# adaLN row products in four column groups of TensorE, and the S5 projection from the first stage on

## Chip, cores, metric

One core of a Trainium2 chip runs the whole layer as one program. The metric is the device time of one execution in microseconds (us), lower is better. The engines are named as in the profile: PE (TensorE), DVE (VectorE), ACT (ScalarE), POOL (GpSimd), and SP, which issues most DMAs. PEld is PE's loading of stationary operands.

## The reference, cut to what matters

The layer takes 512 latent tokens and 256 context tokens of width 2048, all float32. `mod = silu(c) @ ada_w + ada_b` gives six vectors of 2048 for the latent stream: shift and scale of the first norm, gate `g1`, shift and scale of the second norm, gate `g2`. `mod_c`, from `c_ctx`, gives the first two for the context. `ada_w` is 2048 x 12288, so each vector is a row product: one row (or two) against a 2048 x 2048 matrix.

```
h  = modulate(rmsnorm(x), sh1, sc1)                  # 512 x 2048
p  = h @ w_in                                        # S5 takes columns 0:1024, Hyena 1024:4096
ugc = modulate(rmsnorm(ctx), csh1, csc1) @ w_in[:, :1024]
mix = [rmsnorm(S5(p, ugc)), rmsnorm(Hyena(p))]
x  = x + g1 * (mix @ w_out)
h2 = modulate(rmsnorm(x), sh2, sc2)
x  = x + g2 * (silu(h2 @ wg) * (h2 @ wu)) @ wd       # inner width 5632
out = rmsnorm(x)
```

S5 is a diagonal complex scan over the tokens in both directions, Hyena two gated long convolutions by FFT, here by matrix products.

## The kernel before, in words

Activations lie feature-major: a tile is 128 features x 512 tokens. Large products are made in three float32r passes (`mm3`, lines 136-139): weights and activations are split into a high and a low part (`wsplit`, lines 122-134: ACT copies, DVE subtracts), and high-high, high-low and low-high are added in PSUM. Weights come through one `Stream` (lines 141-175): chunks of 512 KB in a fixed order, four raw buffers, loaded by SP three to four chunks ahead, split one ahead.

PE's order is that of the program. Side work is written as generators that yield a cost; `pump(gen, budget)` (lines 188-195) adds the budget to a credit and steps the generator until the credit is used up. The constants `PUMP_...` set how much side work follows each chunk.

The stages in order:

1. **ada** (lines 797-811). For j in 0..3 and kind in 0..1, `ada_block` (760-788) takes 8 chunks of `ada_w`, 2 row tiles (k) of 512 columns each, and makes one matmul for each k (line 766): stationary `sil[:, k, :]` (128 x 2, the silu of c and c_ctx), moving the weights (128 x 512 float32), out 2 x 512. The result is copied by ACT (773) and turned to columns by four small matmuls (778). After each j, `modulate` (790-793) makes the high and low parts of four feature tiles of latent (`hhi`, `hlo`) and context (`chi`, `clo`). Pumped beside: `x_side` (loads and transposes x and ctx, squares, stores `xd`) and `s5_mats`, whose loop b (432-443) makes the S5 input matrices: DVE products, PE transposes into an `ax` PSUM tile, ACT copies into `bm` (one buffer), store to `bmd` by SP.
2. **S5 projection** (868-886): four groups of 256 columns of `w_in`; for each k and 128 columns an "item" of six matmuls, three on 512 latent tokens and three on 256 context tokens, 128 items in all. Pumped beside: the second half of `s5_mats` (448-500), the filter features (503-545), and `late`.
3. **Hyena projection** (1098-1118): 6 groups x 8 chunks x 24 matmuls. Beside it `gen`: the S5 chain (scan on DVE), then `filters`; and `late`.
4. **GLU** (1302-1327): 4 groups x 4 chunks x 24 matmuls, with the rest of `gen`, then `hyena_all`, and `late`.
5. **w_out**, two halves (1336-1391), with `hyena_all` and `late` in the first.
6. **FFN** (1428-1457): gate and up products, then down products, in chunks of eight 128-wide slices; `late` for `g2` in the first chunk.

`late` is `ada_late` (826-862): the other four vectors for the latent stream only (g1, sh2, sc2 by line 865, g2 by line 1409). It has 256 tiles of 128 x 512 of `ada_w`, loaded by SP into three buffers (`araw`, line 835). DVE multiplies each by the scalar `sil[:, k, 0]` and adds it to `acc` (844, 846); after 16 tiles PE sums over the partitions with `ones` (854).

PSUM has eight banks: the pool `mm` has five, `ax` three.

Of the kernel before, what the change touches and what calls it, by code (L numbers as in the profile page):

```python
# [20 lines left out]
L = 512  # L21
# [22 lines left out]
PUMP_BL = 1.8  # L44
PUMP_B = 5.986
PUMP_C = 4.2
PUMP_CL = 1.102
# [4 lines left out]
PUMP_DL = 0.875  # L52
PUMP_EL = 0.619
PUMP_SL = 0.648
PUMP_SC = 0.018
PUMP_FL = 1.826
NRAW = 3
LAG = 0.47
# [14 lines left out]
def kernel(  # L73
# [26 lines left out]
    kp.tile([128, 56], F32, name="padl")  # L100
# [163 lines left out]
    sil = kp.tile([128, KT, 2], F32, name="sil")  # L264
# [48 lines left out]
    def s5_mats():  # L313
# [118 lines left out]
        for b in range(16):  # L432
# [9 lines left out]
            SY.dma_start(bmd[b], bm)  # L442
            yield 3.1
# [22 lines left out]
        for b in range(16):  # L466
# [17 lines left out]
            for gh in range(2):  # L484
# [9 lines left out]
                V.tensor_tensor(out=zg[:, :, 7 * C:8 * C], in0=pz[:C, :, :C], in1=zg[:, :, 7 * C:8 * C], op=ALU.add)  # L494
            zs = Z[:, :, 7 * C:8 * C]
            V.tensor_tensor(out=zs, in0=zs, in1=di, op=ALU.add)
            SY.dma_start(zd[:, gs, :], Z)
            yield 4.4
# [50 lines left out]
    def filters():  # L549
# [112 lines left out]
        for n in range(8):  # L662
# [7 lines left out]
            pump_late(PUMP_SL)  # L670
# [4 lines left out]
            pump_late(PUMP_SL)  # L675
# [21 lines left out]
    rsx = hp.tile([128, L], F32, tag="acc", name="rsx", bufs=1)  # L697
    rsc = hcp.tile([128, CL], F32, tag="rsc", name="rsc", bufs=1)

    def x_side():  # L700
# [12 lines left out]
        for qd in range(4):  # L713
# [5 lines left out]
            for kk in range(4):  # L719
# [6 lines left out]
                SY.dma_start(xd[k], t)  # L726
# [33 lines left out]
    def ada_block(kind, j):  # L760
        ps = mmt(f"ada{kind}_{j}")
        for kc in range(8):
            rw = ws.next()
            for i in range(2):
                k = kc * 2 + i
                T.matmul(ps[:2, :], lhsT=sil[:, k, :], rhs=rw[:, i, :], start=(k == 0), stop=(k == KT - 1))  # L766
            if kc == 2:
                while todo:
                    todo.pop(0)()
            pump(xs, PUMP_X)  # L770
            pump(pre, PUMP_A)
        rowt = tmp(f"rowt{kind}{j}")
        S.copy(rowt[:2], ps[:2, :])

        def columns():
            pc = mmt(f"adc{kind}_{j}")
            for f in range(4):
                T.matmul(pc[:, 2 * f:2 * f + 2], lhsT=rowt[:2, f * 128:(f + 1) * 128], rhs=ident[:2, :2],
                         start=True, stop=True)
# [14 lines left out]

    xs = x_side()
    next(xs)
    for j in range(4):
        for kind in range(2):
            ada_block(kind, j)

        def mods(j=j):
            finish(xs)
            for k in range(4 * j, 4 * j + 4):
                hhi[k], hlo[k] = ht(f"hh{k}", F32R), ht(f"hl{k}", F32R)
                modulate(xT[k], mA[:, k, 0:1], mB[:, k, 0:1], rsx, hhi[k], hlo[k])
# [765 lines left out]
```

## Time and profile before

| | us |
|---|---|
| three runs | 2731.11, 2734.54, 6765.77 |
| median | 2734.54 |
| the profiled execution, device time | 2726.15 |
| its span, first to last instruction | 2724.4 |

The profiled execution is 8.4 us under the median and 5.0 under the lowest run. The page gives busy time by engine, the chain of waits that ended last, groups of instructions and DMA issues; windows give the same by stretch of time. A float32 matmul appears as two records (line 766 has 256 for 128 matmuls); a float32r matmul as one. A record's length on PE contains pipeline time: what a matmul costs in a row of them is the step from one start to the next. "Busy" of PE is therefore above the time that the matmuls need at full pace.

### The profile page before, as it was taken

Reading aid. Unit: us, or ns where it says so; the run is one execution under the profiler, and the core shown is the slowest. Engines: PE = TensorE matmul, PEld = TensorE weight load, DVE = VectorE, ACT = ScalarE, POOL = GpSimd, SP = SyncE. Lnnn points to the kernel's source line nnn. Section 1 sums busy time; section 2 is a strip of 40 time slices with the busy share of each in tenths; the row PEclk is TensorE's granted clock in tenths of the full one; section 3 lists DMA queues with packets and bytes.
Section 4 is the critical chain, followed back from the end, with each engine's and each line's share of the span. In section 5 each row is a group of like instructions: output and inputs, shape, how many; then the busy total and the mean of one; then the engine's idle time right before and its main releaser. Section 6 shows DMA issues by size and latency. Waiting matters only on the chain.

```text
span 2724.4 us, 34481 instructions
## 1 busy us (share of the span) xinstructions
PE 2631.0 (97%) x12431; PEld 2108.4 (77%) x12431; DVE 1517.3 (56%) x2666; ACT 1021.7 (38%) x1869; POOL 116.7 (4%) x143
## 2 busy tenths in 40 slices
PE   7999999999888999999999999999999999999997
PEld 2347777777677888887888888888888888888887
DVE  4779548948859999867463333332333333233338
ACT  5437554564455533233322222222222222222234
POOL 0000010011010001120000000000000000000002
PEclk9999999999999999998999999999999999999999
DMA  8987576676673477443462332333233323332324
GB/s 286 298 270 250 182 229 210 195 240 220 200 237 126 150 216 183 111 155 107 133 205 98 96 99 94 100 93 101 93 101 93 98 96 101 93 101 94 100 93 148
DMA packets 274812, 415.26 MB, mean 152 GB/s; under 512 B 27263, under 2 KB 143279, under 8 KB 274128
## 3 DMA queue, kind: packets, MB, share of 16 engines
q1 hardware_dynamic: 268400, 401.48, 45.4%
q0 software_dynamic: 5664, 10.52, 1.9%
q8 instruction: 98, 1.61, 0.2%
q10 hardware_dynamic: 576, 1.05, 0.1%
q14 instruction: 74, 0.61, 0.1%
HBM read 363.45 MB, written 49.48 MB: 152 GB/s over the span
## 4 chain that ended last, share of the span: by engine, by line
PE 79%; DVE 9%; DMA 5%; ACT 3%; issue 3%; SPq 0%; POOL 0%; DVEq 0%; ACTq 0%; POOLq 0%
PE fg L137 12%; PE fg L138 12%; PE fg L139 12%; PE fd L139 6%; PE fd L137 6%; PE fd L138 6%; PE ada L766 3%; PE wo L138 2%; PE wo L137 2%; PE wo L139 2%; DMA ar<-in_ada_w_dram 1%; PE ph L137 1%; PE ph L138 1%; PE ph L139 1%; PE hi L1219 1%
## 5 line engine op out<-in xcount | busy, mean ns | idle before, releaser
L846 DVE SCALAR_TENSOR_TENSOR acc<-ar,sil,acc 128x512 f32<-128x512 f32 x240 | 180.3, 751 | 60.3 <-DMA ar<-in_ada_w_dram 58.2
L766 PE MATMUL ada<-rad,sil 128*2 128x512 f32 x256 | 121.4, 612 | 14.1 <-DMA rad<-in_ada_w_dram 14.1
L1425 DVE SCALAR_TENSOR_TENSOR xn<-fd,modc,xn 128x512 f32<-128x512 f32 (+1 forms) x112 | 74.6, 672 | 32.3 <-PE fd L139 31.9
L766 PEld LDWEIGHTS ada<-rad,sil 128*2 128x2 f32 x256 | 18.6, 85 | 82.5 <-issue 63.8
L1132 POOL TENSOR_TENSOR sqa<-sqa,sqo 128x256 f32<-128x256 f32 x22 | 19.1, 868 | 1461.5 <-ACT sqo L1131 1460.6
L994 ACT COPY tr<-S 128x128 f32<-128x128 f32 (+1 forms) x96 | 34.0, 362 | 110.7 <-DVE S L998 109.1
L998 DVE TENSOR_REDUCE S<-tr 128x64 f32<-128x192 f32 x190 | 66.4, 350 | 10.0 <-ACT tr L994 5.1
L996 DVE TENSOR_TENSOR tr<-a,S 128x128 f32<-128x128 f32 x190 | 62.5, 329 | 7.3 <-ACT S L961 3.9
L1446 DVE TENSOR_TENSOR ft<-fs,fg 128x512 f32<-128x512 f32 x44 | 30.1, 684 | 61.1 <-PE fg L139 61.1
L1026 POOL DMA_DIRECT2D T<-zd x64 | 37.8, 615 | 532.4 <-ACT u L883 359.7
L1219 PE MATMUL hi<-kiv,cb 128*128 128x256 f32 x256 | 57.2, 380 | 0.4 <-DVE U L1191 0.4
L1219 PEld LDWEIGHTS hi<-kiv,cb 128*128 128x128 f32 x256 | 48.1, 190 | 7.4 <-issue 0.8
L1444 ACT ACTIVATE fs<-fg 128x512 f32<-128x512 f32 x44 | 26.3, 598 | 37.6 <-PE fg L139 37.6
L138 PE MATMUL hf<-zl,ffc 128*128 128x256 f32 x128 | 36.1, 284 | 1.6 <-DVE zl L184 1.6
L137 PE MATMUL hf<-zh,ffc 128*128 128x256 f32 x128 | 37.0, 291 | 0.0
L137 PE MATMUL fdf<-phf,ffc 128*128 128x256 f32 x128 | 36.3, 285 | 0.0
L138 PE MATMUL fdf<-plf,ffc 128*128 128x256 f32 x128 | 36.2, 283 | 0.0
L139 PE MATMUL fdf<-phf,ffc 128*128 128x256 f32 x128 | 36.1, 283 | 0.0
L139 PE MATMUL hf<-zh,ffc 128*128 128x256 f32 x128 | 36.0, 283 | 0.0
L954 PE MATMUL sp<-U,bml 128*128 128x96 f32 x256 | 32.8, 282 | 2.7 <-ACT U L931 2.0
L954 PEld LDWEIGHTS sp<-U,bml 128*128 128x128 f32 x256 | 31.7, 198 | 4.7 <-ACT U L931 2.5
L1449 ACT CAST gh<-ft 128x512 fp32r<-128x512 f32 x44 | 27.2, 619 | 21.6 <-DVE ft L1446 21.6
(3521 smaller groups left out, 8329.3 us busy)
## 6 DMA issues: line engine op xcount, KB each, us to landing
ar<-in_ada_w_dram SPq DMA_DIRECT2D x256, 256.0 KB, 4.0
rwd<-in_ffn_w_down_dram SPq DMA_DIRECT2D x96, 512.0 KB, 3.6
rwf<-in_ffn_w_gate_dram SPq DMA_DIRECT2D x176, 256.0 KB, 2.8
rwf<-in_ffn_w_up_dram SPq DMA_DIRECT2D x176, 256.0 KB, 3.1
rad<-in_ada_w_dram SPq DMA_DIRECT2D x64, 512.0 KB, 5.4
rwv<-in_w_in_dram SPq DMA_DIRECT2D x48, 512.0 KB, 4.9
rwo<-in_w_out_dram SPq DMA_DIRECT2D x32, 512.0 KB, 3.9
bmd<-bm SPq DMA_DIRECT2D x16, 512.0 KB, 3.2
```

The source lines that it names most:

```text
L137: T.matmul(ps, lhsT=wh, rhs=xh, start=start, stop=False)
L138: T.matmul(ps, lhsT=wh, rhs=xl, start=False, stop=False)
L139: T.matmul(ps, lhsT=wl, rhs=xh, start=False, stop=stop)
L766: T.matmul(ps[:2, :], lhsT=sil[:, k, :], rhs=rw[:, i, :], start=(k == 0), stop=(k == KT - 1))
L846: V.scalar_tensor_tensor(out=acc, in0=rw, scalar=sil[:, k, 0:1], in1=acc, op0=ALU.mult, op1=ALU.add)
L954: T.matmul(ps[:, g * NCH:(g + 1) * NCH], lhsT=bm[:, ri, g, :], rhs=U[f4][0][:, hb * 4 + g, :], start=True, stop=True)
L994: S.copy(tr[:, n0:, :, :, 2], St[:, k:k + 2 - n0])
L996: V.tensor_tensor(out=tk[:, :, :, 0:2].rearrange("p r g m -> p m r g"), in0=ac, in1=bc(St[:, k - 1], 2, 2), op=ALU.mult)
L998: V.tensor_reduce(out=St[:, k], in_=tk, op=ALU.add, axis=AX.X)
L1026: GP.dma_start(Tt[:, g, :], bass.AP(zb.tensor, zb.offset, [[C, Q], [G * 240, C], [1, 128]]))
L1219: T.matmul(ps[:, es], lhsT=cbs[s, ft][:, eo, ri, cs], rhs=kiv[:, ft, ri, es], start=(n_ == 0), stop=(n_ == 3))
L1425: V.scalar_tensor_tensor(out=xn[d_][:, cs], in0=pl[f][:, cs], scalar=modc[:, 3, d_:d_ + 1], in1=xn[d_][:, cs], op0=ALU.mult, op1=ALU.add)
```

## The change

- `row_products`: for each k, two matmuls of 256 columns take the place of one of 512. The stationary operand is `silx[:, 2k:2k+32]`, 32 columns of which the first two are wanted. The outputs of the four matmuls of a pair (k even, k odd; left and right half) go to PSUM partitions 0, 32, 64 and 96: four column groups of PE. The small column matmuls sum the two groups that belong together (`sel`).
- `late` uses the same row products: a step takes two tiles, loads two more, and yields 1.0. DVE's lines 844 and 846 and `acc` are gone. There are four `araw` buffers, and `late` starts in the Hyena projection, with one step for each chunk there, two in GLU and in the first half of w_out, one in the FFN's first chunk.
- The S5 projection is taken in two halves of 512 columns, by row tiles: `Half` holds four `mm` banks and, for the first half, two `ax` banks (for the second one `mm` and one `ax`). Two chunks of `w_in` for each of j = 1, 2, 3 come between the `ada_w` chunks; their items (four k tiles x four slices for each j, 48 of the 64 of the first half) run after the row products of `ada` steps, at most two for each step. The items of k = 12 to 15 and the second half follow as before, with `pre` pumped after every two items.
- `modulate` of a j is spread over one k for each step.
- The stores to `bmd` and `xd` are issued by ACT, not SP; `s5_mats` yields between the two halves of a b, in both its loops. `gen` gets 5.0 in place of 4.2 for each chunk of the Hyena projection.

```diff
-NRAW = 3
+NRAW = 4
-PUMP_B = 5.986
-PUMP_C = 4.2
+PUMP_B = 2.4
+PUMP_C = 5.0
...
             ws.add(f"ad{j}{kind}{kc}", (128, 2, 512), [wsrc(adw, kc * 2, 2, kind * D + j * 512, 512)], False)
-    for g in range(4):
-        for kc in range(4):
-            ws.add(f"wi{g}{kc}", (128, 4, 256), [wsrc(win, kc * 4, 4, g * 256, 256)])
+                if j and kind * 8 + kc in (5, 9):
+                    kq = (j - 1) * 4 + kind * 2
+                    ws.add(f"wi0{kq}", (128, 2, 512), [wsrc(win, kq, 2, 0, 512)])
+    for kq in (12, 14):
+        ws.add(f"wi0{kq}", (128, 2, 512), [wsrc(win, kq, 2, 0, 512)])
+    for kq in range(0, 16, 2):
+        ws.add(f"wi1{kq}", (128, 2, 512), [wsrc(win, kq, 2, 512, 512)])
...
-    sil = kp.tile([128, KT, 2], F32, name="sil")
+    silx = kp.tile([128, 64], F32, name="silx")
+    V.memset(silx, 0.0)
+    sil = silx[:, :2 * KT].rearrange("p (k v) -> p k v", v=2)
...
                 S.copy(bm[:, ri], ps.rearrange("p (g c) -> p g c", g=4))
-            SY.dma_start(bmd[b], bm)
-            yield 3.1
+                if ri == 0:
+                    yield 1.5
+            S.dma_start(bmd[b], bm)
+            yield 1.6
...
-                SY.dma_start(xd[k], t)
+                S.dma_start(xd[k], t)
...
+    def row_products(ps, k0, tiles):
+        for i, rw in enumerate(tiles):
+            k = k0 + i
+            lhs = silx[:, 2 * k:2 * k + 32]
+            for ch in range(2):
+                q = k % 2 * 2 + ch
+                T.matmul(ps[q * 32:(q + 1) * 32, :256], lhsT=lhs, rhs=rw[:, ch * 256:(ch + 1) * 256],
+                         start=(k < 2), stop=(k >= KT - 2))
...
-    def ada_block(kind, j):
+    def ada_block(kind, j, fill):
         ps = mmt(f"ada{kind}_{j}")
         for kc in range(8):
             rw = ws.next()
-            for i in range(2):
-                k = kc * 2 + i
-                T.matmul(ps[:2, :], lhsT=sil[:, k, :], rhs=rw[:, i, :], start=(k == 0), stop=(k == KT - 1))
-            if kc == 2:
-                while todo:
-                    todo.pop(0)()
+            row_products(ps, kc * 2, [rw[:, i, :] for i in range(2)])
+            if kc >= 2 and todo:
+                todo.pop(0)()
+            fill(kind * 8 + kc)
             pump(xs, PUMP_X)
             pump(pre, PUMP_A)
...
+    class Half:
...
+        def open(self):
+            h = self.h
+            self.pl = [mmt(f"pl{h}{f}") for f in range(4)]
+            px = [mmt(f"pcx{h}0") if h else axt(f"pcx{h}0"), axt(f"pcx{h}1")]
+            self.pc = [px[f // 2][:, f % 2 * 256:f % 2 * 256 + 256] for f in range(4)]
...
+        def run(self, n):
+            while n and self.todo:
+                k, f, wh, wl = self.todo.pop(0)
+                mm3(self.pl[f], wh, wl, hhi[k], hlo[k], k == 0, k == KT - 1)
...
+                n -= 1
...
+        def fill(step, j=j):
+            if j and step in (5, 9):
+                half.rows((j - 1) * 4 + (2 if step == 9 else 0))
+            half.run(2 if step < 13 else 1)
...
+    half.run(100)
     while todo:
         todo.pop(0)()
...
-        for i, (vi, j, k) in enumerate(steps):
-            rw = raws.pop(i)
+        for i in range(0, len(steps), 2):
+            vi, j, k = steps[i]
             if k == 0:
-                acc = hp.tile([128, 512], F32, tag="acc", name=f"acc{vi}{j}", bufs=1)
-                V.tensor_scalar(out=acc, in0=rw, scalar1=sil[:, k, 0:1], scalar2=None, op0=ALU.mult)
-            else:
-                V.scalar_tensor_tensor(out=acc, in0=rw, scalar=sil[:, k, 0:1], in1=acc, op0=ALU.mult, op1=ALU.add)
+                ps = mmt(f"adl{vi}{j}")
+            row_products(ps, k, [raws.pop(i), raws.pop(i + 1)])
             load(i + NRAW)
-            yield 0.6
...
+            load(i + NRAW + 1)
+            if k == KT - 2:
+                rowt = tmp(f"rowl{vi}{j}")
+                S.copy(rowt[:, :256], ps[:, :256])
+                yield 1.0
...
+    for h in range(2):
+        if h:
+            half = Half(1)
+        for kq in range(0 if h else 12, 16, 2):
+            half.rows(kq)
+            for n in range(4):
+                half.run(2)
+                pump(pre, PUMP_B)
+        half.close()
...
             pump(gen, PUMP_C)
-            pump(late, PUMP_CL)
+            pump(late, 1)
...
-            if hy:
-                pump(late, PUMP_DL)
+            pump(late, 2)
...
         pump(hy, PUMP_D)
-        pump(late, PUMP_DL)
-
-    while not done_g1:
-        pump(late, 0.1)
+        pump(late, 2)
...
-                if f0 or g:
-                    pump(late, PUMP_FL)
+                pump(late, 1)
```

## Rows read from the trace of the kernel before

**Rows 1.** The page: the span, and busy time of PE, DVE and ACT.

```profile
span 2724.4 us, 34481 instructions
...
PE 2631.0 (97%) x12431; PEld 2108.4 (77%) x12431; DVE 1517.3 (56%) x2666; ACT 1021.7 (38%) x1869; POOL 116.7 (4%) x143
```

**Rows 2.** Windows by stage; columns in the first line.

```profile
core 0: us, PE busy (x) PEld busy (x) DVE busy (x) ACT busy (x) POOL busy (x), PEclk, DMA share, GB/s
0.00:186.00 186.00, 166.40 (x594) 56.97 (x595) 115.41 (x239) 83.76 (x179) 0.70 (x6) 0.98 0.87 296
186.00:361.00 175.00, 173.83 (x934) 136.19 (x933) 131.37 (x262) 105.74 (x257) 0.02 (x1) 1.00 0.67 209
361.00:744.00 383.00, 355.86 (x1755) 292.69 (x1755) 280.25 (x645) 213.16 (x387) 31.82 (x53) 0.98 0.67 215
744.00:944.00 200.00, 178.73 (x954) 150.20 (x954) 163.51 (x221) 111.40 (x186) 22.54 (x27) 0.97 0.52 172
944.00:1165.00 221.00, 217.14 (x1191) 189.37 (x1190) 199.64 (x350) 67.13 (x125) 25.80 (x24) 1.00 0.60 171
1165.00:1255.00 90.00, 83.60 (x378) 69.89 (x377) 53.87 (x82) 28.15 (x49) 16.73 (x12) 0.95 0.40 138
1255.00:1435.00 180.00, 179.90 (x794) 149.04 (x795) 103.59 (x159) 58.46 (x95) 0.00 (x0) 0.98 0.49 157
```

**Rows 3.** Chain that ended last, in order: start us, us, engine, line, records.

```profile
156.00 3.52 PE ada L766 x8
...
159.52 1.02 PE bt L440 x8
...
201.94 3.65 DMA ar<-in_ada_w_dram
...
264.84 3.58 PE zp L488 x16
...
406.52 3.75 PE sp L954 x32
```

**Rows 4.** Timeline of PE in the FFN's down products: start us, us.

```profile
1479.69 0.39 PE L137 MATMUL fd<-gh,swd0020h 128*128 128x512 f32 x1
...
1480.37 0.39 PE L137 MATMUL fd<-gh,swd0020h 128*128 128x512 f32 x1
```

**Rows 5.** Timeline of PE in the S5 projection: one item, and the next.

```profile
188.37 0.40 PE L137 MATMUL pl<-hh,swi00h 128*128 128x512 f32 x1
...
189.42 0.40 PE L137 MATMUL pl<-hh,swi00h 128*128 128x512 f32 x1
```

**Rows 6.** Windows of 15 us in the first stage; columns as in rows 2.

```profile
60.00:75.00 15.00, 15.00 (x44) 3.95 (x44) 3.07 (x13) 1.96 (x5) 0.00 (x0) 1.00 0.98 345
...
120.00:135.00 15.00, 14.79 (x51) 4.51 (x49) 12.65 (x24) 5.21 (x10) 0.00 (x0) 1.00 0.95 326
```

**Rows 7.** Waits: who waited for whom, us in total, times, longest.

```profile
DVE acc L846 <- DMA ar<-in_ada_w_dram: 58.2, 50, 5.4
...
ACT bm L441 <- DMA bmd<-bm: 39.3, 12, 5.3
```

**Rows 8.** Waits of SP's queue; columns as in rows 7.

```profile
SPq L835 <- DVE acc L846: 79.0, 103, 7.3
...
SPq L442 <- ACT bm L441: 35.3, 15, 3.7
```

**Rows 9.** Windows by stage of line 846 alone (DVE).

```profile
361.00:744.00 383.00, 78.98 (x105) 0.98 0.67 215
...
1255.00:1435.00 180.00, 33.76 (x45) 0.98 0.49 157
```

**Rows 10.** DMA issues of the page: count, KB each, median us to landing.

```profile
ar<-in_ada_w_dram SPq DMA_DIRECT2D x256, 256.0 KB, 4.0
...
bmd<-bm SPq DMA_DIRECT2D x16, 512.0 KB, 3.2
```

**Rows 11.** Window of tile yp (S5 readout) in the GLU stage.

```profile
744.00:944.00 200.00, 19.82 (x73) 14.91 (x72) 5.14 (x14) 0.97 0.52 172
```

More of the change, by code (lines that the diff above doesn't have):

```diff
@@ L793, in modulate, with __init__, rows, close @@
         V.scalar_tensor_tensor(out=lo, in0=t, scalar=B, in1=hi.bitcast(F32), op0=ALU.add, op1=ALU.subtract)
+    class Half:
+        def __init__(self, h):
+            self.h, self.pl, self.todo = h, None, []
+        def open(self):
[3 more added lines that the diff above has]
+            self.pc = [px[f // 2][:, f % 2 * 256:f % 2 * 256 + 256] for f in range(4)]
+        def rows(self, kq):
+            if self.pl is None:
+                self.open()
+            wsp = ws.next()
+            for i in range(2):
+                k = kq + i
+                for f in range(4):
+                    self.todo.append((k, f, *(t_[:, f * 128:(f + 1) * 128] for t_ in wsp[i])))
+        def run(self, n):
+            while n and self.todo:
+                k, f, wh, wl = self.todo.pop(0)
+                mm3(self.pl[f], wh, wl, hhi[k], hlo[k], k == 0, k == KT - 1)
+                T.matmul(self.pc[f], lhsT=wh, rhs=chi[k], start=(k == 0 and f % 2 == 0), stop=False,
+                         skip_group_check=True)
+                T.matmul(self.pc[f], lhsT=wh, rhs=clo[k], start=False, stop=False, skip_group_check=True)
+                T.matmul(self.pc[f], lhsT=wl, rhs=chi[k], start=False, stop=(k == KT - 1), skip_group_check=True)
+                n -= 1
+        def close(self):
+            for f in range(4):
+                fi = self.h * 4 + f
+                u1, u2 = tmp(f"u1{fi}"), tmp(f"u2{fi}")
+                S.copy(u1, self.pl[f])
+                V.tensor_copy(u2[:, :CL], self.pc[f])
+                SY.dma_start(ud[fi, :, CL:], u1)
+                SY.dma_start(ud[fi, :, :CL], u2[:, :CL])
@@ L795, with mods @@
     xs = x_side()
     next(xs)
+    half = Half(0)
     for j in range(4):
+        def fill(step, j=j):
+            if j and step in (5, 9):
+                half.rows((j - 1) * 4 + (2 if step == 9 else 0))
+            half.run(2 if step < 13 else 1)
         for kind in range(2):
-            ada_block(kind, j)
-        def mods(j=j):
+            ada_block(kind, j, fill)
+        def mods(k):
             finish(xs)
-            for k in range(4 * j, 4 * j + 4):
-                hhi[k], hlo[k] = ht(f"hh{k}", F32R), ht(f"hl{k}", F32R)
-                modulate(xT[k], mA[:, k, 0:1], mB[:, k, 0:1], rsx, hhi[k], hlo[k])
-                chi[k], clo[k] = hct(f"ch{k}", F32R), hct(f"cl{k}", F32R)
-                modulate(cT[k], mA[:, k, 1:2], mB[:, k, 1:2], rsc[:, :CL], chi[k], clo[k])
@@ L809 @@
-        todo.append(mods)
+            hhi[k], hlo[k] = ht(f"hh{k}", F32R), ht(f"hl{k}", F32R)
+            modulate(xT[k], mA[:, k, 0:1], mB[:, k, 0:1], rsx, hhi[k], hlo[k])
+            chi[k], clo[k] = hct(f"ch{k}", F32R), hct(f"cl{k}", F32R)
+            modulate(cT[k], mA[:, k, 1:2], mB[:, k, 1:2], rsc[:, :CL], chi[k], clo[k])
+        for k in range(4 * j, 4 * j + 4):
+            todo.append(lambda k=k: mods(k))
+    half.run(100)
     while todo:
@@ L860, in ada_late @@
                                            in1=VC["n2g"][:, ks], op0=ALU.add, op1=ALU.mult)
[L861 to L864 removed]
+            else:
+                yield 1.0
     late = ada_late([0, 1, 2])
[L868 to L886 removed]
+    for h in range(2):
[7 more added lines that the diff above has]
+        half.close()
     hcp.release()
@@ L896, in yg_split @@
         split(src, *yg[k])
-    def pump_late(n):
-        pump(late, n)
     def s5_chain():
```

66 lines of the change are left out of this document (16 added, 50 removed).

## The prediction

> **What bounds the kernel now.** I read the page first: PE is busy for 97% of the span, DVE for 56% [rows 1]. That share alone doesn't settle it, since a PE record is longer than what it costs, so I priced the records by their steps. In the FFN three float32r matmuls of 512 columns start 0.68 us apart: 0.227 each [rows 4]. A float32 record of 512 columns takes 3.52 / 8 = 0.44 us, one of 256 columns 3.58 / 16 = 0.22, short ones 3.75 / 32 = 0.117 to 1.02 / 8 = 0.128 [rows 3]. An item of the S5 projection takes 1.05 us [rows 5].
>
> With these, and the counts in the windows [rows 2], each stage shows what PE needs and what is free:
> - ada, 0 to 186: 256 records of line 766 (113 us) and 338 short ones (43): 156, 30 free. But the DMA engines have a share of 0.87 there at 296 GB/s, and where they are full they move 326 to 345 GB/s [rows 2, 6]. This stage stands at the DMA limit as much as at PE's.
> - S5 projection, 186 to 361: 128 items (134), 128 records of 0.22 (29), 38 short ones (4): 167, 8 free. PE's own work.
> - Hyena projection, 361 to 744: 1152 matmuls (261), some 120 readout records (27), 483 short (57): 345, 38 free. DVE is busy for 280 here, 79 of it in line 846 [rows 2, 9], and over the whole kernel it stands 58 us before that line waiting for `ar` [rows 7]: in this stage DVE makes PE wait.
> - GLU, 744 to 944: 384 matmuls (87), 64 of the filters (15), 73 readout records (16) [rows 11], 433 short ones or half-width ones at 0.115 (50): 168, 32 free.
> - w_out, 944 to 1255: 768 (174), 256 at 0.22 (57), 545 at 0.115 (63): 294 of 311, 17 free.
> - FFN: the first chunk's gate and up have 768 matmuls (174) in 180 us [rows 2]. Nothing is free to the end.
>
> So work taken off PE in the first stage gives nothing until DMA follows; work put on PE in the last one costs all of it; between them DVE's relief gives back part.
>
> **The set of four.** Everything hangs on what one set of `row_products` costs: four matmuls of 256 columns, eight records of 0.22 us. The trace has no matmul beside another in a different column group. The bounds: if nothing overlaps, 8 x 0.22 = 1.76 us. If all four run together, the two records of one remain, 0.44 us. Each matmul is two records for the same column group, and records start one after the other in the trace. If a start has to wait for the one before it, the second record of a group holds up the next group, and only two groups run at a time: 5 x 0.22 = 1.10 us for a set alone, 4 x 0.22 = 0.88 in a series. I take 1.0: between these two, as half of the sets stand alone between wide matmuls.
>
> The Trainium skill speaks for this order: "TensorE: Matmul & The Clock Gate", Part 3, says that column tiles run concurrently, but also that matmuls start and end strictly in program order. It speaks against the change elsewhere: "TensorEngine Tiling (Array Packing)", Key Properties, says that changing the tiling mode drains the array. Here 104 pumps put sets between wide matmuls. In this trace eight short records between narrow ada matmuls took 1.02 us against 0.94 by the pace of a run of short ones [rows 3]; if that 0.08 were such drains, the sum would be 8 us higher.
>
> **Part by part, the changes in us.**
>
> ada: 0. PE's need falls from 113 to 64 sets x 0.88 = 56 and rises by the 48 items moved in (50): 156 becomes 149. DMA: 186 us at 296 GB/s are 55 MB, six more chunks of 512 KB make 58; at the 326 GB/s of a full window [rows 6] 178 us, and 8 for the thin first slices. SP is freed of its 35 us of waits for `bm` [rows 8], since ACT issues that store behind its own copy; the 32 issues that ACT takes over stand in front of its row and `modulate` copies, and its 102 us of free time cover them. If the DMA engines can be kept at 345, up to 10 are gained; if PE can't overlap sets, the stage becomes 156 + 50 = 206. The items' weight splits (six chunks, four splits of ACT and DVE each) lie beside, as both engines have 70 us or more free [rows 2].
>
> S5 projection: -42. 48 items x 1.05 leave (-50), and 16 short records of `late` (-2). What is late next: the first items now need the feature tiles k = 12 to 15 at once, where before the first group began with k = 0. Last ada copy, column matmuls, and the three `modulate` steps are some 7 us without cover; the change of halves, with four banks to empty at once, 3. Line 846's 45 passes here were off the path. The price of the moved yields is nothing as long as ACT (106 of 175 busy) keeps up in 133: it would be at three quarters.
>
> Hyena projection: +49. 48 sets (+48). `gen` gets 240 units in place of 202, so the rest of the S5 chain comes forward from GLU: 73 readout records (16), short ones (2), and 22 of the filters' 120 units (11 of 62): +29. The generator loads its first tiles and uses them in the same step; PE waits for that landing, 4.0 us median [rows 10]: +4. Two fewer column tables than before in this stage: -2. Later loads have two chunks of lead, 14 us, and cost nothing; if SP is held up, a late pair now stops PE and not DVE. DVE loses 79 us of work and its waits for `ar`, so of the 38 free us I leave 8: -30. Bounds: 0 to -38.
>
> GLU: -19. The work that came forward leaves (-29), 32 sets arrive (+32), the wait for the last S5 output and DVE's hold are mostly gone: 32 free becomes 10 (-22; bounds 0 and -32).
>
> w_out: +11. 16 sets (+16), free time 17 to 12 (-5), as DVE stays nearly full with the Hyena products.
>
> FFN: +36. 32 sets (+32) and the first load (+4), all on the path: DVE did this in 34 us [rows 9] beside PE, with 104 of 180 busy [rows 2]. Nothing hides it.
>
> Sum: 0 - 42 + 49 - 19 + 11 + 36 = +35. The profiled execution took 2726.15, so 2761. The two nearest of the runs shown lie 5 and 8 us above that execution; the range holds this.
>
> **The rivals.**
> 1. All four groups run together, 0.5 us a set with its fill. For it: the outputs lie in four separate partition groups, and the order of the four is made so that neighbours differ. Against: each matmul is two records in one group. 128 late sets x 0.5 less: 2761 - 64 = 2697. The Trainium skill's "TensorEngine Tiling (Array Packing)", Theoretical Speedup, gives up to four times for 32 columns, which is this case; no run shows it yet.
> 2. Nothing overlaps, the change doesn't do what it says: 1.76 a set. 128 x 0.76 = +97, and ada rises to 206, +20: 2878. For it: every pair of records in the trace so far follows at full distance. Against: all those use the same columns.
> 3. Slower at any set price: the first two stages gain nothing. The first half holds four `mm` and two `ax` banks, so the next ada block waits for ACT's copy of the last one, and the S5 matrices have one `ax` bank in place of three. ACT stood 39 us waiting for `bmd` to land, 3.2 us each [rows 7, 10]; with one bank every such wait reaches PE, and through the raw buffers DMA. Price: the 42 us, 2761 + 42 = 2803. It decides once copy and store take longer than the pumps between two halves of a b, about 3 us. Against: the new yields put items between, and the raw buffers cover some us.
>
> **How the numbers follow.** Forecast 0.45, own range 2730 to 2800; rival 1 0.31; rival 2 0.08; rival 3 0.16. Within 2% of the median (2680 to 2789) is about what a measurement of this kernel can't tell from no change. Faster by more: two in five of rival 1, when more free time goes, and a little of the rest: 0.15. Slower: rival 2 (0.08), two thirds of rival 3 (0.10), a fifth of the forecast (0.08): 0.26. The rest, 0.59. The range of 8 in 10 runs from rival 1 with somewhat more free time, 2688, to 2840, short of rival 2.
>
> **What would show it.** Starts of a set's eight records: last to first plus one record is 1.1 us if I am right, 0.5 for rival 1, 1.8 for rival 2. The first fg of the FFN to its first fd: 216 us, not 180. ada's last row product at 180 to 195, its DMA share above 0.9. The S5 projection some 130 us long; over 150 with PE waiting for ACT copies, or ada over 200 with a share below 0.87, is rival 3. Line 846's waits are gone, the Hyena projection is near 430 and GLU near 180. A Hyena stage that still has 30 us free would say that DVE was not what held PE there.

## The result, and the profile after

The changed kernel takes 2852.02 us, median of four runs (2846.11 to 2859.06); the kernel before, beside it, 2734.08 (also of four; one of them took 6765.77). The ratio is 1.0436, 95% interval 1.0405 to 1.0468: clearly slower. The forecast was 2761 in a range of 2688 to 2840, so the time lies above the range, near rival 2, whose mechanism is not what happened.

The page of the changed kernel: span, busy time of the engines, one group of part 5 and two issues of part 6.

```profile
span 2848.7 us, 36746 instructions
...
PE 2690.4 (94%) x13711; PEld 2146.3 (75%) x13711; DVE 1373.5 (48%) x2421; ACT 1028.4 (36%) x1877; POOL 111.4 (4%) x143
...
L768 PE MATMUL adl<-ar,silx 128*32 128x256 f32 x1024 | 83.3, 392 | 0.0
...
ar<-in_ada_w_dram SPq DMA_DIRECT2D x256, 256.0 KB, 3.9
...
rad<-in_ada_w_dram SPq DMA_DIRECT2D x64, 512.0 KB, 5.0
```

Against [rows 1] the span is 124 us longer, and DVE has lost 144 us of work without PE's idle time getting smaller: 2848.7 - 2690.4 = 158 us now, 2724.4 - 2631.0 = 93 before.

Windows of the changed kernel by stage, cut at the last row product of ada and at the first matmul of each later stage (S5 projection, Hyena projection, GLU, the two halves of w_out, the first chunk of the FFN).

```profile
core 0: us, PE busy (x) PEld busy (x) DVE busy (x) ACT busy (x) POOL busy (x), PEclk, DMA share, GB/s
0.00:208.30 208.30, 157.74 (x1116) 100.88 (x1116) 124.80 (x252) 87.83 (x186) 0.70 (x6) 0.89 0.80 274
208.30:354.40 146.10, 130.59 (x654) 95.75 (x647) 90.66 (x194) 95.83 (x239) 0.00 (x0) 0.92 0.45 145
354.40:859.60 505.20, 448.27 (x2360) 343.52 (x2358) 259.01 (x588) 254.24 (x454) 43.94 (x74) 0.93 0.57 184
859.60:1046.80 187.20, 180.42 (x1137) 143.91 (x1137) 144.54 (x212) 90.94 (x152) 8.60 (x6) 0.99 0.65 216
1046.80:1238.10 191.30, 188.31 (x1110) 160.37 (x1109) 144.13 (x250) 52.81 (x99) 16.80 (x17) 1.00 0.55 158
1238.10:1350.50 112.40, 102.08 (x455) 84.21 (x453) 68.80 (x107) 33.07 (x58) 23.11 (x18) 0.96 0.44 134
1350.50:1558.00 207.50, 205.46 (x1057) 151.78 (x1057) 72.03 (x109) 59.23 (x97) 0.00 (x0) 0.99 0.49 155
```

These answer to [rows 2]. Cut in the same way, the kernel before has 183, 178, 388, 194, 312 (both halves of w_out) and 180. So ada is 25 longer and the S5 projection 32 shorter, the Hyena projection is 117 longer, GLU and w_out are 7 and 8 shorter, and the first chunk of the FFN is 28 longer. The rest of the FFN is unchanged. The Hyena projection is where most of the loss stands, though part of its 117 us is work of GLU and w_out that moved there, as e6 shows below.

Waits of PE in the changed kernel's Hyena projection: who waited for whom, us in total, times, longest.

```profile
PE ph L129 <- ACT rowl L916: 26.4, 5, 11.9
PE h3f L598 <- DVE w3sf L591: 10.4, 2, 5.5
PE u2p L994 <- ACT S L1014: 8.4, 12, 1.3
```

The first row is a wait that the kernel before doesn't have: the next matmul into an `mm` bank stands until ACT has copied a finished late row out of one. One of the five, from the timeline of PE and of ACT:

```profile
439.46 0.64 PE L768 MATMUL adl<-ar,silx 128*32 128x256 f32 x8
444.69 0.79 PE L129 MATMUL ph<-hh,swv10h 128*128 128x512 f32 x1 [4.59 <-ACT rowl L916]
445.28 0.63 PE L130 MATMUL ph<-hl,swv10h 128*128 128x512 f32 x1
445.71 0.63 PE L131 MATMUL ph<-hh,swv10l 128*128 128x512 f32 x1
...
453.39 0.63 PE L130 MATMUL ph<-hl,swv10h 128*128 128x512 f32 x1
453.81 0.54 PE L131 MATMUL ph<-hh,swv10l 128*128 128x512 f32 x1
454.19 0.40 PE L129 MATMUL ph<-hh,swv11h 128*128 128x512 f32 x1
454.43 0.39 PE L130 MATMUL ph<-hl,swv11h 128*128 128x512 f32 x1
```

```profile
439.76 0.36 ACT L1044 COPY tr<-S 128x128 f32<-128x128 f32 x1 [1.57 <-DVE S L1048]
441.34 0.36 ACT L1044 COPY tr<-S 128x128 f32<-128x128 f32 x1 [1.22 <-DVE S L1048]
442.91 0.36 ACT L1044 COPY tr<-S 128x128 f32<-128x128 f32 x1 [1.21 <-DVE S L1048]
443.12 1.12 ACT L123 CAST swv11h<-rwv 128x512 fp32r<-128x512 f32 x2
444.27 0.37 ACT L916 COPY rowl<-adl 128x256 f32<-128x256 f32 x1
```

The row is finished at 440, but its copy stands in ACT's queue behind copies of the S5 scan, each of which waits 1.2 us or more for DVE's step, and behind a weight split. It starts at 444.27, and PE has idled 4.59 us. After that the same records start 0.43 us apart in place of 0.23, until 454: TensorE runs at the lower of its two levels there, 1.2 GHz, as the granted clock of these two windows says (1.00 before the pause, a mean of 0.74 with it):

```profile
425.00:440.00 15.00, 15.00 (x82) 10.68 (x80) 13.66 (x38) 5.06 (x14) 0.00 (x0) 1.00 0.48 143
440.00:460.00 20.00, 15.41 (x61) 12.03 (x58) 14.78 (x38) 7.37 (x16) 0.00 (x0) 0.74 0.39 130
```

What took 9.5 us from 444.69 would have taken about 9.5 x 0.227 / 0.43 = 5.0 at the full level, so a pause of 4.6 us cost PE another 4.5.

### The profile page after: what moved, and what is told of

Same layout as the page of the kernel before. It is cut to its first block, busy times and chain, and to the rows that moved or that the text cites. A ratio compares the mean times of both kernels' runs of the same rounds, so it can differ in the third digit from the quotient of the medians.

```text
span 2848.7 us, 36746 instructions
## 1 busy us (share of the span) xinstructions
PE 2690.4 (94%) x13711; PEld 2146.3 (75%) x13711; DVE 1373.5 (48%) x2421; ACT 1028.4 (36%) x1877; POOL 111.4 (4%) x143
## 4 chain that ended last, share of the span: by engine, by line
PE 59%; DVE 1%; issue 0%; DMA 0%; ACT 0%; POOL 0%; DVEq 0%; POOLq 0%; ACTq 0%
PE fg L129 11%; PE fg L130 11%; PE fg L131 11%; PE fd L131 6%; PE fd L129 6%; PE fd L130 6%; PE wo L129 2%; PE wo L130 2%; PE wo L131 2%; PE hi L1267 1%; PE adl L768 1%; DMA xd<-xp 0%; PE hf L129 0%; PE hf L131 0%; PE hf L130 0%
## 5 line engine op out<-in xcount | busy, mean ns | idle before, releaser
L768 PE MATMUL adl<-ar,silx 128*32 128x256 f32 x1024 | 83.3, 392 | 0.0
L768 PE MATMUL ada<-rad,silx 128*32 128x256 f32 x512 | 53.3, 449 | 20.1 <-DMA rad<-in_ada_w_dram 11.9
L768 PEld LDWEIGHTS adl<-ar,silx 128*32 128x32 f32 x1024 | 23.2, 108 | 36.0 <-issue 27.7
L439 ACT COPY bm<-bt 128x512 f32<-128x512 f32 x32 | 18.8, 587 | 75.1 <-DMA bmd<-bm 45.2
L768 PEld LDWEIGHTS ada<-rad,silx 128*32 128x32 f32 x512 | 14.3, 120 | 39.3 <-DMA rad<-in_ada_w_dram 16.2
L488 PE MATMUL zp<-R,bst 128*48 128x256 f32 x128 | 33.0, 402 | 6.2 <-DVE Z L494 5.5
```

Of the source, the lines that this page charges most:

```text
L488: T.matmul(psz[:48, g * 256:(g + 1) * 256], lhsT=bsf[:, b * 2 + gh, g * C:g * C + 48], rhs=R[:, gg].rearrange("p d j c -> p (d j c)"), sta ...
L768: T.matmul(ps[q * 32:(q + 1) * 32, :256], lhsT=lhs, rhs=rw[:, ch * 256:(ch + 1) * 256], start=(k < 2), stop=(k >= KT - 2))
```

## What a late set costs: two edits on the sets themselves

The timeline of PE in the changed kernel's FFN, around one set; then a series of three sets in ada.

```profile
1377.55 0.50 PE L129 MATMUL fg<-xh,swf004h 128*128 128x512 f32 x1
...
1382.90 0.39 PE L131 MATMUL fg<-xh,swf004l 128*128 128x512 f32 x1
1383.22 0.64 PE L768 MATMUL adl<-ar,silx 128*32 128x256 f32 x8
1383.79 0.50 PE L129 MATMUL fg<-xh,swf005h 128*128 128x512 f32 x1
```

```profile
156.57 1.50 PE L768 MATMUL ada<-rad,silx 128*32 128x256 f32 x24
```

Eight records together last 0.64 us where one lasts 0.39, so the last starts about 0.25 after the first, one record's pace of 0.22: all four groups run together, and only the two records of one matmul follow each other. In a series eight more records add (1.50 - 0.64) / 2 = 0.43 us. That is the lower bound of the prediction, 0.44, on which rival 1 stood, and not my 1.0. But alone between wide matmuls a set costs more: from one chunk's start to the next is 1383.79 - 1377.55 = 6.24 us, of which the 24 wide matmuls are 24 x 0.227 = 5.45. The set is the other 0.79: 0.43 for its records and 0.36 for going in and out.

A change of form had its price in the kernel before, too, between the ada matmuls (stationary operand 128 x 2) and the S5 matrices' transposes (128 x 128), without the four groups:

```profile
155.93 3.59 PE L766 MATMUL ada<-rad,sil 128*2 128x512 f32 x8
159.46 0.65 PE L440 MATMUL bt<-ident,imb 128*128 128x128 f32 x4
159.95 0.60 PE L440 MATMUL bt<-ident,reb 128*128 128x128 f32 x4
160.48 1.45 PE L766 MATMUL ada<-rad,sil 128*2 128x512 f32 x3
```

The eight records of ada start 0.43 us apart among themselves, but 3.53 us pass until the first transpose, 0.09 more than eight steps; the eight transposes start 0.11 us apart, but 1.02 us pass until the next ada matmul, 0.14 more. So about 0.23 us for out and in again, before any change.

**e8_few_sets.** Three quarters of the late sets left out.

```
-            row_products(ps, k, [raws.pop(i), raws.pop(i + 1)])
+            pair = [raws.pop(i), raws.pop(i + 1)]
+            if k in (0, KT - 2):
+                row_products(ps, k, pair)
```

> The changed kernel with 96 of the 128 late sets left out: of every group of eight sets only the first and the last are multiplied, so that the late vectors are incomplete; loads, row copies, column matmuls and yields stay. Theory (the late sets cost PE their own time, 0.87 us each between wide matmuls in the FFN, as that stage's 28 us for 32 sets show): 96 sets less are 72 to 84 us, so 2765 to 2780, and the chunk of the FFN with 24 sets less falls from 208 to about 187. Rival (what costs is not the sets but the waits around them, for the row copies and the bank): over 2810, with the chunk of the FFN still above 200.

Measured: 2808.95 us, 1.0267 [1.0252, 1.0281], between the two, 1 us short of the rival's. The FFN chunk, 207.5 to 189.0, is the theory's: 24 sets less, 0.77 each. From the Hyena projection to the end of w_out 72 sets less gave only 27 us (996 to 969), and the waits of PE for the row copies stayed in the Hyena projection (28.0 us, 26.4 with all sets). So in the FFN the sets are nearly the whole cost (32 x 0.77 = 25 of 28 us), and before it there is another one.

**e9_four_tiles.** The same sets, two of them at each place.

```
-        for i in range(0, len(steps), 2):
+        for i in range(0, len(steps), 4):
...
-            row_products(ps, k, [raws.pop(i), raws.pop(i + 1)])
+            row_products(ps, k, [raws.pop(i + n) for n in range(4)])
...
-                yield 1.0
+                yield 2.0
```

> The changed kernel with the late steps taken two sets at a time (16 records one after the other, half as many places between wide matmuls, the same sets and loads). Theory (0.43 us of a set's 0.87 are its records, as in the series of ada; the rest, some 0.4, is paid once per place, going in and out): 64 places less, -16 in the stage of the FFN's first chunk x 0.4 = -6.4, so 208 becomes 201 to 202; in all 2848.7 - 64 x 0.4 = about 2823, less what loads that are now two at a time cost: 2823 to 2840. Rival (a set costs 0.87 whatever stands before it): the chunk stays at 207 to 209 and the whole at 2845 to 2855.

Measured: 2830.92, 1.0358 [1.0337, 1.038]; the FFN chunk takes 199.7, a little under the theory's 201 to 202; the whole is in its range. Here are two sets in the FFN, from the timeline of PE:

```profile
1356.95 0.39 PE L131 MATMUL fg<-xh,swf002l 128*128 128x512 f32 x1
1357.27 1.07 PE L768 MATMUL adl<-ar,silx 128*32 128x256 f32 x16
1358.27 0.50 PE L129 MATMUL fg<-xh,swf003h 128*128 128x512 f32 x1
```

Going in and out is paid once for both: from the set's start to the next wide matmul 1.00 us in place of twice 0.57. Half of the 32 places less took 7.8 us off this stage, 0.49 each with what goes with them. In the Hyena projection the wait of `ph` for the row copies nearly goes (1.4 us, where the changed kernel has 26.4), yet PE idles 52 us of that stage, as against 57: other copies are now the last that it waits for.

## Where the late products run, and how fast the generator is pumped

**e1_late_dve** puts the late products back on DVE, with the pumps of before, and keeps all else. **e6_gen_budget_4_2** is the changed kernel with the Hyena stage's generator budget of before. **e7_late_dve_4_2** has both.

```
-PUMP_C = 5.0
+PUMP_C = 4.2
```

```
-            row_products(ps, k, [raws.pop(i), raws.pop(i + 1)])
+                V.tensor_scalar(out=acc, in0=rw, scalar1=sil[:, k, 0:1], ...
+                V.scalar_tensor_tensor(out=acc, in0=rw, ...
...
-            pump(late, 1)
+            pump(late, PUMP_CL)
```

> Only the late row products go back to DVE, with the budgets of before; ada in column groups, the early S5 items and the ACT stores stay. Theory (most of the loss is the late products on PE: 29 us in the FFN's first chunk, and in the Hyena projection the sets themselves plus waits of PE for ACT's copy of the late row behind the scan's copies, with a lower clock after each): FFN chunk 180, Hyena projection 390 to 410, total 2720 to 2750. Rival (the first stage and the banks of the early S5 items carry half of the loss): total 2780 or more, ada still 213.

> The changed kernel with the budget of gen in the Hyena projection back at 4.2. Theory (5.0 puts 5.8 scan steps of 0.76 us and 2.5 us of splits on ACT and DVE for each chunk, more than PE's 5.4 to 6.2 us, so that each group's end finds both late, PE pauses and its clock falls): Hyena projection and GLU together 692 to about 640, total 2795 to 2815. Rival (the sets on PE and the bank they hold make the stage long, whatever the budget): Hyena and GLU together 680 or more, total within 15 of 2852.

> Late products on DVE and the budget of gen at 4.2: of the change only the ada groups, the early S5 items by halves and the ACT stores are left. Theory (the two causes together are the whole loss behind the S5 projection): Hyena and GLU together 582 to 595 as before, total 2715 to 2735. Rival (the halves or the stores delay the S5 chain too): Hyena and GLU 620 or more, total 2755 or more.

Measured: e1 2777.27, 1.0154 [1.0139, 1.017]; e6 2835.11, 1.0373 [1.035, 1.0396]; e7 2753.13, 1.0075 [1.0053, 1.0098]. All three lie between their theory and their rival. In e1 the FFN chunk falls to 178.5, as expected, but the Hyena projection takes 480, not 390 to 410. In e6 Hyena projection and GLU take 441 + 211 = 652, in e7 409 + 195 = 604. One window for each kernel from the first Hyena matmul to the end of w_out: before, changed, e6, e7 (columns as above).

```profile
361.20:1255.30 894.10, 835.34 (x4274) 702.07 (x4272) 697.57 (x1296) 419.93 (x747) 96.69 (x115) 0.98 0.59 187
```

```profile
354.40:1350.50 996.10, 919.08 (x5056) 732.01 (x5054) 616.49 (x1154) 431.07 (x762) 92.45 (x115) 0.96 0.57 180
```

```profile
353.10:1336.80 983.70, 920.40 (x5054) 731.06 (x5053) 616.58 (x1154) 435.78 (x766) 93.38 (x115) 0.96 0.58 180
```

```profile
366.50:1283.10 916.60, 844.00 (x4279) 706.34 (x4277) 706.51 (x1320) 423.60 (x750) 96.99 (x115) 0.97 0.60 187
```

PE's idle time is the length less its busy time: 59 us before, 77 in the changed kernel. e7 has 73 us idle, e6, with the 96 sets of these stages on PE and 90 us less on DVE, 63. PE's busy time rose by 76, 0.80 a set, as the FFN's chunk step says; the relief of DVE gave back 9. With the larger budget on top (changed, against e6) PE has the same busy time and 77 us idle. So the budget costs 12 in these stages, and in e1 against e7 it costs 29. With the larger budget the relief gave back 15 (e1 has 92 us idle, the changed kernel 77). Of the 57 us that I took as gained by DVE's relief 9 to 15 were there, net of the new waits for row copies.

The budget moves more work than it costs: from e6 to the changed kernel the Hyena projection grows from 441 to 505, while GLU falls from 211 to 187 and w_out from 332 to 304. In e1 no row copy is made by ACT, and the pauses are at the filters' features in place of it; the first of three such rows from e1's Hyena projection, 26 us together (e7 has 3.4):

```profile
PE h3f L606 <- ACT cv L1177: 14.9, 1, 14.9
```

**e2_swap** pumps the late step ahead of the generator in a Hyena chunk; **e3_late_in_ax** takes the late row's bank from `ax`.

```
-            pump(gen, PUMP_C)
             pump(late, 1)
+            pump(gen, PUMP_C)
```

```
-                ps = mmt(f"adl{vi}{j}")
+                ps = axt(f"adl{vi}{j}")
```

> In each chunk of the Hyena projection the late step is emitted before gen's steps and not after, nothing else. Theory (PE waits for the late row's copy because it stands in ACT's queue behind six scan steps of the same chunk): waits for rowl fall from 26 us to under 10, the low clock after them goes, Hyena projection 504 to about 455, total 2800 to 2815. Rival (the stage is long because gen's larger budget of 5.0 makes ACT and DVE late for everything): within 15 us of 2852.

> The late row's PSUM bank comes from the pool of three, not from the pool of five that the wide products use. Theory (the bank held until ACT copies it is what stops the next Hyena group): wide products no longer wait for rowl, total 2800 to 2820. Rival (the S5 chain needs the three banks itself, and its transposes then wait): S5 transposes wait for rowl instead, total above 2840.

Measured: e2 2854.13, 1.0431 [1.0411, 1.0451], no difference; e3 2847.11, 1.0414 [1.0398, 1.0429], whose interval overlaps the changed kernel's. The waits of PE, first in e2, then in e3:

```profile
PE ph L129 <- ACT rowl L916: 21.6, 5, 9.4
```

```profile
PE adlc L920 <- ACT rowl L916: 15.9, 3, 10.4
```

Neither the order of the two pumps nor the pool of the bank changes the time: with another bank PE stops at the column matmuls of the same row. Both were misses for the idea that the place of the wait is the cost. That the copy comes late because of what stands before it in ACT's queue is what the timeline at 440 us shows for one pause; for the others it is argued.

**e14_fours_42** joins e9 and e6 (their two edits).

> The changed kernel with late sets two at a time and the generator's budget at 4.2 together; alone they gave 21 and 17 us. Theory (two separate costs of PE's time): 2852 - 38, 2810 to 2820, the chunk of the FFN 199 to 201. Rival (both act on the same waits in the Hyena stage): 2825 to 2835.

Measured: 2826.83, 1.034 [1.0322, 1.0358]: the rival. The FFN chunk keeps its 7 us (200), but from the Hyena projection to the end of w_out it is 19 us shorter than the changed kernel, where e6 alone is 12 and e9 alone 17. That these are the same waits is the rival's reading; no wait was followed to show it. Against e9 the budget is worth 4 us here, within the two intervals.

## The first two stages

**e4_no_early** leaves all S5 items behind ada, with the pump of the matrices scaled to the greater number of steps (1.5 for 2.4).

```
-            if j and step in (5, 9):
-                half.rows((j - 1) * 4 + (2 if step == 9 else 0))
-            half.run(2 if step < 13 else 1)
+            pass
...
-        for kq in range(0 if h else 12, 16, 2):
+        for kq in range(0, 16, 2):
```

> All items of the S5 projection come after the ada stage, in the same two halves by row tiles; ada keeps its column groups. Theory (in the ada stage PE waits for ACT with one free bank in the small pool, and DMA is not fed): ada 170 to 180 with a DMA share above 0.9, S5 projection 185 to 195, total 2855 to 2875 (little changed). Rival (the early items cost more than they bring): total below 2840. If column groups don't help the ada stage: ada stays at 186 or more.

**e10_one_ax_free** gives the first half one `ax` bank less, **e12_early_loads_only** leaves the 48 early items' products out and keeps their loads and splits.

```
-            px = [mmt(f"pcx{h}0") if h else axt(f"pcx{h}0"), axt(f"pcx{h}1")]
+            px = [mmt(f"pcx{h}0"), axt(f"pcx{h}1")] if h else [axt(f"pcx{h}0")] * 2
...
+                if f > 1 and not self.h:
+                    continue
```

```
+                k0 = 0 if self.h else 12
+                if k < k0:
+                    continue
+                mm3(self.pl[f], wh, wl, hhi[k], hlo[k], k == k0, k == KT - 1)
```

> The changed kernel with the context part of the S5 projection's first half cut to its slices 0 and 1 (slices 2 and 3 are not multiplied, so that part of the S5 input is missing), by which the first half holds one ax bank in place of two and ada has two to turn over. Left out are 32 items' context products, 96 records of 0.22 us = 21 us of PE's work, 18 of them in ada. Theory (the one ax bank, through ACT's wait for the landing of bm, holds PE and the raw tiles in ada): ada falls from 208 to 175 to 188, more than the 18 us of records. Rival (ada is held by its load traffic, or by PE's own work): 190 to 206, no more than the records.

> The changed kernel with the products of the 48 early items left out (288 records of 512 and 288 of 256 columns; k = 0 to 11 of the first half are missing in the S5 input); their loads, weight splits and banks stay in ada. Theory (PE pays for the early items in ada, 208 - 164 = 44 us, since nothing of its idle time there takes them): ada 160 to 172, S5 projection unchanged at 143 to 148, in all 2800 to 2814. Rival (the extra loads and splits, or the bank held, make ada longer): ada 185 to 208, in all over 2822.

Measured: e4 2848.6, 1.0431 [1.0405, 1.0457]; e10 2830.99, 1.0346 [1.0327, 1.0365]; e12 2826.53, 1.0344 [1.0321, 1.0367]. Lengths of ada and of the S5 projection: changed 208 + 146, e4 164 + 191, e10 196 + 136, e12 180 + 149. Their ada windows, in the order e4, e12:

```profile
0.00:164.00 164.00, 105.29 (x812) 57.58 (x812) 105.56 (x224) 77.18 (x170) 0.70 (x6) 0.82 0.91 323
```

```profile
0.00:179.90 179.90, 111.27 (x816) 56.92 (x816) 120.52 (x248) 85.57 (x184) 0.70 (x6) 0.80 0.91 314
```

In both the DMA share is 0.91, so the loads hold these two, and moving the items' chunks, splits and banks forward costs 180 - 164 = 16 us. With the products as well the share falls to 0.80 at 208 us: another 28 us, in which neither PE (158 of 208 busy) nor DMA is full. Items that start early make ada longer by what the S5 projection gets shorter: 208 + 146 = 354, and 164 + 191 = 355. e4's ada is shorter than its theory had it, and its time does not differ from the changed kernel's. In e12 ada lies between theory and rival, and the whole on the rival's side (over 2822): both had a part. To judge by: the same ada code took 206 to 214 us in the profiles of nine of these kernels.

e10 doesn't bear out the bank: ada takes 196, where the theory wanted 188 at most. But the test is weaker than I made it. In the trace a context record starts 0.12 us after the one before it, not 0.22, so what was left out is 72 x 0.12 = 9 us in ada and 12 in all; ada became 12 shorter and the whole 21. Some 3 us in ada, and up to 9 in all, may be the bank's, a small part of the 42 that rival 3 gave it. What the trace shows besides is SP's queue, here the waits of the weight stream for PE to let go of a raw tile, in ada, changed, then e12, then e4:

```profile
SPq L147 <- PE ada L768: 106.8, 48, 5.8
```

```profile
SPq L147 <- PE ada L768: 65.5, 46, 5.8
```

```profile
SPq L147 <- PE ada L765: 66.0, 44, 6.8
```

A raw tile comes free when its row products have run, and these now stand behind items in PE's queue. That reading fits the three runs, but it is not shown: no kernel with more raw tiles was run. PE also ran at the lower clock for part of ada (mean granted clock 0.89, where the kernel before had 0.98); what that costs there stays open.

**e5_before_ada_groups** is the kernel before with the column groups in ada alone; **e11_before_ada_act** adds ACT's stores and the split yield of the first loop.

```
-                T.matmul(ps[:2, :], lhsT=sil[:, k, :], rhs=rw[:, i, :], start=(k == 0), stop=(k == KT - 1))
+            row_products(ps, kc * 2, [rw[:, i, :] for i in range(2)])
```

```
-            SY.dma_start(bmd[b], bm)
-            yield 3.1
+                if ri == 0:
+                    yield 1.5
+            S.dma_start(bmd[b], bm)
+            yield 1.6
...
-                SY.dma_start(xd[k], t)
+                S.dma_start(xd[k], t)
```

> The kernel before with one part of the change: row products in four column groups in the ada stage only. Theory (the column groups relieve the ada stage and what follows stays as it was): ada 164 to 170, S5 projection 178 to 182, total 2712 to 2722, ratio 0.99 to 0.996. Rival (the 20 us come back in the S5 projection, since pre then has had less time): total 2730 to 2740.

> The kernel before with three parts of the change in its first stage alone: the column groups in the ada row products, the stores of bm and of the x features issued by ACT, and the yield between the two parts of a bm. Theory (with the S5 items not in it, ada falls to 164 as in the changed kernel without early items; with the column groups alone it was 175): ada 160 to 168, S5 projection unchanged at 179, in all 2708 to 2716. Rival (the queue of the stores doesn't matter without early items): 2722 to 2728 as with the column groups alone.

Measured: e5 2725.1, 0.9974 [0.9959, 0.9989], ada 175 and the S5 projection 179; e11 2726.69, 0.997 [0.9959, 0.998], ada 164 and the S5 projection 191. Both are 0.3% below the kernel before, a small difference, but neither interval holds 1. e5 lies between theory and rival. e11 is a miss: the stores and the split yield do take ada to 164, but 13 of the 19 us come back in the next stage.

**e13_dve_42_no_early** is e7 without early items (the edits of e7 and e4; the late steps in the S5 projection at 0.45).

> The changed kernel with the late products back on VectorE, the generator's budget at 4.2 and no early S5 items (all 128 after ada; the late steps per item scaled from 0.72 to 0.45, so that as many run in the S5 projection): of the change there remain the column groups in ada, the row tiles of the S5 projection and the stores from ACT. Theory (the 20 us that version still loses in the Hyena stage come from the early items, by what they push together behind them): Hyena 388 to 395, in all 2718 to 2732, as the kernel before with the column groups and ACT stores in ada. Rival (they come from something else in the changed S5 stage or in the shared banks): Hyena 403 to 412, in all 2745 to 2756.

Measured: 2737.58, 1.001 [0.9995, 1.0024]. The Hyena projection takes 395 us, which is the theory's; e7 had 409. The whole is 6 us over its range: ada takes 171, not 164, and GLU 199. From the Hyena projection to the end of w_out the kernel before takes 894 us, e13 906, e7 917: the early items cost 10 us behind the S5 projection, by which wait was not followed.

## Why the prediction was wrong

By the profiled executions the forecast was +35 and the measured change +124, 89 more. Sorted by stages and by the runs that part them:

| where | forecast | measured | missed by |
|---|---|---|---|
| ada and S5 projection | -42 | -7 | 35 |
| Hyena projection to w_out: early items, row tiles, stores (e7 against before) | 0 | +23 | 23 |
| the same stages: late sets and DVE's relief (e6 against e7) | +41 | +67 | 26 |
| the same stages: the generator's budget (changed against e6) | 0 | +12 | 12 |
| first chunk of the FFN | +36 | +28 | -8 |

The step that failed by most is the S5 work moved into ada. It was to bring 42 us and brought nothing: with the early items the first two stages take 354 us, without them 355 (e4). Behind them come 23 more, 10 of which are the early items' own (e7 against e13). Then comes DVE's relief, 48 short, of which the cheaper sets take back 20 in these stages; then the budget, 12.

Undone one at a time, the parts make a ladder. Each is a ratio to the kernel before, times 2734:

| kernel | ratio | step, us |
|---|---|---|
| before | 1 | |
| e11, column groups and ACT's stores in ada | 0.997 | -8 |
| e13, and the row tiles of the S5 projection | 1.001 | +11 |
| e7, and the early items | 1.0075 | +18 |
| e6, and the late sets on PE | 1.0373 | +81 |
| changed, and the generator's budget of 5.0 | 1.0436 | +17 |

The runs stand in several batches, each beside the kernel before. e13 also holds the changed buffers and pumps, so its +11 belongs to no one line. That the late sets cost +81, where the forecast's terms for them add to about +75 (128 for the sets, 8 for first loads, -4 for short records, -57 for the relief), is luck: sets priced too high and a relief priced too high nearly cancel.

**The set's price: the reason fell, the sum nearly stood.** I had 1.0 us, because I took it that a matmul's second record holds up the next group. It doesn't: a series costs 0.43. What made 0.79 of it is the step that I priced at 0.08 and left out of the sum, the change between the narrow and the wide form. The Trainium skill's "TensorEngine Tiling (Array Packing)", Key Properties, says that changing the tiling mode drains the array; the trace agrees that a change costs, with 0.36 us for in and out. Whether it is a drain that is paid, no run separates. My 0.08 came out too small: the pace of 0.117 that I held against the transposes contains such ends itself, and the 0.09 on their other side went into the 0.44; read by starts, as above, it is about 0.23. So the FFN's term, +36, measured +28, for another reason than mine, and by the price of the 128 late sets alone the time would have come out 27 us under the forecast.

**DVE's relief: a step that failed.** I took 30 us back in the Hyena projection, 22 in GLU and 5 in w_out, 57 in all, because DVE had stood 58 us before line 846 [rows 7] and I read PE's free time there as waits for DVE. e6 against e7 shows 9, the changed kernel against e1 15. DVE's waits for `ar` were its own: no wait of PE names line 846. Of PE's idle time in those stages (894.1 - 835.3 = 59 us before) the waits put 31 us down to DVE and 20 to ACT; in the Hyena projection, where I took 30, they give DVE 14, most of it the copies that empty the banks at a group's end. First the kernel before, then e6:

```profile
PE ph L137 <- DVE cv L1116: 13.1, 8, 3.1
```

```profile
PE ph L129 <- ACT rowl L916: 17.0, 4, 6.3
```

In e6 DVE's wait is gone, and the late row's copy by ACT, for which the sum has no term, stands in its place; in e9, where PE hardly waits for that copy, `cv` is back with 9.1 us. At a group's end PE waits for several copies, and each view names the last. The prediction named the sign of this: a Hyena stage that still has 30 us free. It has 57.

**The generator's budget: the term that was missing.** I counted 240 units in place of 202 as work that comes forward and leaves GLU by as much: +29 and -29. Work did come forward (GLU has no `yp` record left, where [rows 11] had 73), but GLU got only 7 us shorter. This costs 17 us with the late sets on PE (e6), 22 with them on DVE (e1 against e7), 4 with the sets two at a time (e14 against e9, not clear of noise). I had no term for what closer steps do to ACT and DVE. In the changed kernel PE pauses for row copies, as at 440 us, in e1 for the filters' features; that both come late because ACT and DVE get more work for a chunk than PE's chunk lasts is argued, not shown.

**ada: 0 forecast, +25 measured; the S5 projection: -42 forecast, -32 measured.** The term for the loads was right: I gave 178 and 8 to the DMAs, and with loads alone e12 takes 180. The failed step is that PE's 149 us of work would fit beside them: with the products the stage takes 208. In the S5 projection PE now idles 16 of 146 us, where it idled 1 of 178. Rival 3 had this time for these stages, the first two stages gaining little, but e10 leaves its bank a few us. That the early items also cost time behind the S5 projection (e7 against e13) had no term at all; its mechanism stays open.

**w_out: +11 forecast, -8 measured.** The generator's larger budget took work out of it: with the old one (e6) it takes 332.

By the rivals: 1 was right on how the groups run and wrong on the cost of a set among wide matmuls, 2 came nearest in time (2878) with a mechanism that the trace excludes, and 3 was right that the first stages gain next to nothing. None had a cost of the early items behind their stage, DVE's relief at a quarter, or the budget at a price.

## What to carry to other kernels

Price narrow matmuls by where they stand: in a series these sets cost 0.43 us, one at a time between wide ones 0.79, so put them together or leave them where PE is not the bound. Before crediting an engine's relief, look whether the bound engine's idle time names that engine: 90 us off DVE gave PE 9 to 15 us here. Work moved into the idle time of a stage at its load limit may not find that time: here ada went from 180 to 208 us with products that were to fit beside its loads.

## What was not expected of the hardware

Four float32 matmuls of 256 columns in four column groups take 0.43 us, as long as the two records of one [rows 3]: full overlap. The change between these sets and wide matmuls costs about 0.36 us for in and out; between 128 x 2 and 128 x 128 operands in the kernel before it was about 0.23. After a pause of 4.59 us that followed uninterrupted work at the full level, the granted clock fell to the lower level, and records stepped 0.43 us apart for 9 us. In ada, with PE busy for 105 of 164 us (e4), the mean granted clock was 0.82, where the kernel before with its slower row products had 0.98 [rows 2]: the work that is left there runs in part at the lower level.
